# Norm factors folded into small per-token scalars, and another order of loads, splits and modulation matmuls at six seams of a two-layer backbone

## The chip, the cores and the metric

One core of a Trainium2 chip runs the whole program. The metric is the device time in microseconds (us), the median of the timed executions shown below. TensorE is named PE in the profile, VectorE DVE, ScalarE ACT, GpSimd POOL; SP is the engine whose queue issues most loads and stores.

## The reference, cut to what matters

512 tokens (256 context, 256 latent) of width 1024 pass through two layers. What the change touches of each layer:

```python
ml = adaln(c, w_ada[l], b_ada[l])                # six modulation rows: shift, scale, gate, twice
hl = modulate(rmsnorm(xl, norm1_g[l]), ml[0], ml[1])
# token mixing: three branches of one input projection, merged by sigmoid gates
q = rmsnorm(q, qn_g); k = rmsnorm(k, kn_g)       # (A) attention, per head half of 64
s = q @ k.T * 64 ** -0.5;  p = softmax(s)
q = l2norm(q) * 128 ** -0.5;  k = l2norm(k)      # (B) gated DeltaNet, per head of 128
kb = k * beta;  l_mat = strict(kb @ k.T * decay) # then a chunked scan with q, k, v, beta, g
y = rmsnorm(o, norm_g) * silu(z)
y = gates[0] * (ys[0] @ w_branch[0]) + gates[1] * (ys[1] @ w_branch[1]) + gates[2] * (ys[2] @ w_branch[2])
xl = xl + ml[2] * (y @ w_out)
hl = modulate(rmsnorm(xl, norm2_g[l]), ml[3], ml[4])
xl = xl + ml[5] * peer_ffn(hl, ...)              # product-key experts
```

Layer 1 needs the latent tokens alone behind its keys and values, so most of its blocks are 256 columns wide where layer 0 has 512.

## The kernel before, in words

Activations lie transposed, features on partitions and tokens along the free dimension. Each matrix product is three fp32r matmuls (`mm3`, L101 to L103): the operand is split into a high part (an ACT cast, L94) and a rest (a DVE subtraction, L97). `wblock` (L119) loads one weight block of 512 KB and splits it; `tblock` (L133) multiplies it with the hidden state `hh`, `hl`.

`run` (L1289) goes through a layer in this order. **Start**: `norm_sums` (squares and column sums of x), the modulation blocks (`ada`, L175: four loads of 512 KB, 8 matmuls on the two condition vectors, a copy on ACT, a fold of four small matmuls), the small parameters (`mix_params`), then `hmod` (L203), which takes the reciprocal root of the sums, spreads it over the partitions by two matmuls (`rowb`, L499 and L500) and makes `hh` and `hl`. **Mixer** (L226): `gdn_gates`, then `weave` mixes three streams of work: the DeltaNet groups (two heads each, `gdn_group`), the recurrent and attention heads with `merge_early` behind them, and a list of fillers, merge gates and `ada` blocks. How many units of the others follow each DeltaNet unit is a table (`RATE`, L267), which the change leaves alone. **Merge** (L930): the DeltaNet branch output, which lies in memory as `ysd[1]`, is loaded (`yraw`), split and projected, summed with the other two (`y`, `ya`) under the gate `mth`, and projected with `w_out` onto x. **Second norm**: `hmod` again with `ada` blocks 10 and 11. Then queries, routing and experts.

Norm factors in the mixer are per token, and a token is a column there. `cols_rsqrt` leaves them as one column of scalars per 128 tokens; `rowsb` (L461) spreads such columns to a full tile by one 128x128 fp32 matmul per 128 tokens (L470), and DVE multiplies. `sq_cols` (L448) forms the sums of squares by an ACT square and one matmul with one column out per 128 tokens (L454).

The engines work their rows in order; the recording layer places the rows of each engine. The DMA queue of SP takes loads in the order of its rows. Weight loads share three buffers (`wraw`).

## Time and profile before

| what | value |
|---|---|
| time, median of 3 runs | 4547.12 us (4546.77 to 4556.1) |
| time of the profiled execution | 4536.66 us |
| its span | 4535.0 us |
| mean granted TensorE clock | 0.969 of 2.4 GHz |
| busy: PE, DVE, ACT, POOL | 4283.0 (94%), 3214.4 (71%), 2348.0 (52%), 457.7 (10%) us |

The profiled execution is 10.5 us shorter than the median, so sums are made against 4536.66 and carried over to 4547.12. The stretches of its span, in us: start 0 to 65, mixer of layer 0 to 1177, merge to 1294, second norm to 1322, queries, routing and experts to 2606; start of layer 1 to 2648, mixer to 3550, merge to 3622, second norm to 3641, the rest to 4535. Busy shares are averages over these; at the borders PE stands still. Those borders are called seams here.

### The profile page before, as it was taken

The page shows a single profiled execution, that of the slowest core. Times are in us where ns is not written, and L with a number is a line of the kernel's source. Part 1 is how long each engine was busy: PE and PEld are TensorE (multiplying, and loading weights), DVE is VectorE, ACT ScalarE, POOL GpSimd, SP SyncE. Part 2 cuts the span into 40 slices and gives each one's busy share as a digit, 9 for nine tenths or more (in the row PEclk, how much of TensorE's full clock was granted, in tenths as well). Part 3 has the DMA queues.
Part 4 walks back from the last instruction along what each step waited for, and adds up shares of the span by engine and source line. Part 5 has one row for each costly group of instructions (what it writes and reads, how often), then busy time and mean ns, then how long its engine had stood idle before and what let it go on. Part 6 is the DMA issues. An engine that isn't in the chain of part 4 may idle for free.

```text
span 4535.0 us, 67054 instructions
## 1 busy us (share of the span) xinstructions
PE 4283.0 (94%) x24379; PEld 3612.7 (80%) x24379; DVE 3214.4 (71%) x7412; ACT 2348.0 (52%) x4145; POOL 457.7 (10%) x444
## 2 busy tenths in 40 slices
PE   7999999999889999999999989989998899999999
PEld 4686877777668999988888856878776789988888
DVE  4767576764459998677888766777775588656665
ACT  4555555553244688433333354656554357854444
POOL 0000000000000222333444200000000001100000
PEclk8999999999989999999999989999998999999999
DMA  4313222225632688899999734223221746677775
GB/s 152 121 59 109 70 96 86 96 73 175 205 107 91 235 275 294 320 333 336 338 340 333 251 121 140 84 84 98 66 89 57 236 149 208 228 266 243 242 248 182
DMA packets 364604, 820.69 MB, mean 181 GB/s; under 512 B 67184, under 2 KB 187504, under 8 KB 360944
## 3 DMA queue, kind: packets, MB, share of 16 engines
q1 hardware_dynamic: 315568, 614.00, 41.4%
q0 software_dynamic: 45824, 160.46, 9.7%
q10 hardware_dynamic: 2880, 41.94, 2.4%
q8 instruction: 191, 3.13, 0.3%
q14 instruction: 141, 1.16, 0.1%
HBM read 715.62 MB, written 100.66 MB: 180 GB/s over the span
## 4 chain that ended last, share of the span: by engine, by line
PE 81%; DVE 10%; ACT 4%; DMA 4%; issue 1%; SPq 0%; ACTq 0%; DVEq 0%
PE mm L103 11%; PE mm L101 11%; PE mm L102 11%; PE acx L101 4%; PE acx L102 4%; PE acx L103 4%; PE px L101 3%; PE px L102 3%; PE px L103 3%; DVE wl L97 2%; PE acg L103 1%; PE acg L101 1%; PE px L872 1%; PE acg L102 1%; PE pg L102 1%; PE pg L101 1%
## 5 line engine op out<-in xcount | busy, mean ns | idle before, releaser
L101 PE MATMUL mm<-hh,wh 128*128 128x256 f32 (+2 forms) x2784 | 916.2, 329 | 38.9 <-ACT wh L94 26.7
L103 PE MATMUL mm<-hh,wl 128*128 128x256 f32 (+2 forms) x2784 | 908.9, 327 | 18.6 <-DVE wl L97 18.3
L102 PE MATMUL mm<-hl,wh 128*128 128x256 f32 (+2 forms) x2784 | 903.5, 325 | 0.0
L94 ACT CAST wh<-wraw 128x1024 fp32r<-128x1024 f32 (+2 forms) x473 | 487.6, 1033 | 660.6 <-PE mm L102 525.2
L97 DVE TENSOR_TENSOR wl<-wraw,wh 128x1024 fp32r<-128x1024 f32 (+2 forms) x473 | 566.8, 1199 | 231.9 <-ACT wh L94 229.8
L101 PEld LDWEIGHTS mm<-hh,wh 128*128 128x128 f32 x2784 | 533.2, 192 | 68.9 <-ACT wh L94 28.5
L103 PEld LDWEIGHTS mm<-hh,wl 128*128 128x128 f32 x2784 | 531.9, 191 | 49.3 <-DVE wl L97 29.9
L102 PEld LDWEIGHTS mm<-hl,wh 128*128 128x128 f32 x2784 | 533.2, 192 | 22.9 <-issue 2.5
L97 DVE TENSOR_TENSOR vl<-vraw,vh 128x1024 fp32r<-128x1024 f32 x256 | 313.0, 1223 | 142.3 <-ACT vh L94 139.6
L94 ACT CAST vh<-vraw 128x1024 fp32r<-128x1024 f32 x256 | 269.0, 1051 | 274.4 <-PE pg L103 164.7
L94 ACT CAST pah<-ge 128x384 fp32r<-128x384 f32 (+1 forms) x256 | 114.7, 459 | 225.3 <-DVE ge L1196 172.0
L1160 DVE TENSOR_SCALAR ob<-cst,iT 128x128 f32<-128x128 f32 x640 | 183.3, 347 | 66.1 <-PE pg L1161 22.1
L1013 POOL DMA_DIRECT2D early<-ge x160 | 89.3, 558 | 1355.5 <-ACT ge L1006 952.3
L1218 POOL DMA_INDIRECT grow<-in_v,gix x128 | 179.5, 1403 | 259.4 <-DVE gacc L1233 229.6
L101 PE MATMUL mm<-hh,whx 128*128 128x512 f32 (+1 forms) x544 | 202.9, 373 | 2.9 <-ACT tx L800 1.8
L103 PE MATMUL mm<-hh,wlx 128*128 128x512 f32 (+1 forms) x544 | 200.9, 369 | 2.1 <-DVE wlx L97 2.1
L102 PE MATMUL mm<-hl,whx 128*128 128x512 f32 (+1 forms) x544 | 201.3, 370 | 0.0
L101 PE MATMUL px<-vh,pah 128*128 128x512 f32 x512 | 199.5, 390 | 0.0
L102 PE MATMUL px<-vl,pah 128*128 128x512 f32 x512 | 199.5, 390 | 0.0
L103 PE MATMUL px<-vh,pal 128*128 128x512 f32 x512 | 199.2, 389 | 0.0
L1218 POOL DMA_INDIRECT grow<-in_ur,gix x128 | 161.4, 1261 | 269.8 <-DVE gdot L1224 163.0
L1233 DVE SCALAR_TENSOR_TENSOR gacc<-grow,gdot,gacc 128x1024 f32<-128x1024 f32 x127 | 163.3, 1286 | 1.5
(518 smaller groups left out, 10030.3 us busy)
## 6 DMA issues: line engine op xcount, KB each, us to landing
wraw<-in_u SPq DMA_DIRECT2D x256, 512.0 KB
vraw<-in_v SPq DMA_DIRECT2D x256, 512.0 KB
wraw<-in_win SPq DMA_DIRECT2D x192, 512.0 KB
wraw<-in_wada SPq DMA_DIRECT2D x96, 512.0 KB
gate<-st ACTq DMA_DIRECT2D x20, 2048.0 KB
wraw<-in_wbr SPq DMA_DIRECT2D x48, 512.0 KB
pgt<-gate SPq DMA_DIRECT2D x32, 768.0 KB
wraw<-in_wq SPq DMA_DIRECT2D x32, 512.0 KB
```

The source lines that it names most:

```text
L94: self.S.copy(h, src)
L97: return self.V.tensor_tensor(l, src, h.bitcast(F32), ALU.subtract)
L101: mm(out, lh, rh, start=first, stop=False)
L102: mm(out, lh, rl, start=False, stop=False)
L103: mm(out, ll, rh, start=False, stop=last)
L872: T.matmul(sc, a[s, q0:q0 + P], b[s, :nk], start=t == 0, stop=t == 2)
L1013: self.nc.gpsimd.dma_start(hd[j], self.expert_h(gl, l, j, T0, N))
L1160: ob = V.tensor_scalar(b, iota, iT[:, 1, n + k:n + k + 1], iT[:, 2, n + k:n + k + 1], ALU.is_equal, ALU.mult)
L1218: nc.gpsimd.indirect_dma_start(r, None, table, bass.IndirectOffsetOnAxis(ap=ix[:, k:k + 1], axis=0))
L1233: V.scalar_tensor_tensor(acc, r, dot[:, k:k + 1], acc, ALU.mult, ALU.add)
```

## The change

**DeltaNet.** The keys stay raw: their squared norm factor goes into beta (`bt`, `nbt`, `nb0`, 8 or 16 columns wide), its root into the value tile (`dv`, by a DVE multiply in place of an ACT copy). The query factor goes into the epsilon of the output norm (`qe`), since that norm divides it out again. The output `o` is formed with tokens on partitions (`qg` and `QK` become the weights of its matmuls), so the output norm's factor is a scalar per partition: ACT squares 128 columns at a time with a running sum, ACT scales 128 columns at a time, PE transposes back, and one DVE operation in place of two applies gain and gate. The blocks of a group come as k0, k1, q0, v0, q1, v1.

**Attention.** The query gain is applied by the ACT copy out of PSUM, and the query factor times 0.125 is the softmax scale, so that queries need no `rowsb`.

**Seams.** The first load of x is in 8 parts; the modulation blocks at the start have 8 buffers of their own. The gate weights and the first weight block behind each `hmod` are loaded and split ahead of it. Blocks 4, 5 and 10, 11 (of both layers) come as a `fill` behind the second `rowb` matmul; blocks 4 and 5 of layer 0 leave the mixer's filler list for that. In `merge` the loads of `yraw` come first, then `ya`, then x; `yraw` has 4 buffers in layer 0 and 8 in layer 1.

```diff
+    def preload(self, dram):
+
+        self.pre = self.wblock(dram)
...
+        if self.pre:
+            w, self.pre = self.pre, None
+            return w
...
-            w = self.t(self.wp, [P, 2, 512], F32, "wraw", 3)
+            w = self.t(pool, [P, 2, 512], F32, "adaw", 8) if pool else self.t(self.wp, [P, 2, 512], F32, "wraw", 3)
...
+        fp = self.tc.tile_pool(name=self.nm("fill"), bufs=1, reuse_waits="tile")
+        with fp as p, self.tc.issue_after(self.lastrow.ins):
+            for b in fill:
+                self.ada(l, b, p)
...
-            ad = [lambda a=a: self.ada(*a) for a in ([(0, b) for b in range(4, 10)] + [(1, b) for b in range(4)] if l == 0 else [(1, b) for b in range(6, 10)])]
+            ad = [lambda a=a: self.ada(*a) for a in ([(0, b) for b in range(6, 10)] + [(1, b) for b in range(4)] if l == 0 else [(1, b) for b in range(6, 10)])]
...
+            if w < 2:
+                self.sq_cols(dst, ss[:, sc[w][hh]:], self.ones[:, :1])
+            if w:
+                pt = self.px()
+                for c in range(4):
+                    T.transpose(pt[:, c * P:(c + 1) * P], dst[:, c * P:(c + 1) * P], idt)
+                if w == 1:
+                    S.copy(kN[:, hh].rearrange("p a b -> p (a b)"), pt)
                 else:
-                    dst = (kT if w else qT)[:, hh]
-                    V.scalar_tensor_tensor(dst, th, 1.0, cv, ALU.add, ALU.mult)
-                    self.sq_cols(dst, ss[:, sc[w][hh]:], self.ones[:, :1])
+                    V.tensor_tensor(vN[:, hh], v4(pt), dv[:, 4 * hh:4 * hh + 4].unsqueeze(2).to_broadcast([P, 4, P]), ALU.mult)
+            if (hh, w) == (1, 1):
+                k2, dv = c1("k2"), c1("dv")
+                V.tensor_scalar(k2, ss[:, :8], 1.0, 4 * EPS, ALU.mult, ALU.add)
+                rk = self.rsqrt(self.sp, k2, "rq")
+                V.scalar_tensor_tensor(dv, k2, 0.5, rk, ALU.mult, ALU.mult)
+                V.tensor_tensor(k2, rk, rk, ALU.mult)
+                bt, nbt, nb0 = mk([P, 2, 4, 2], "bt", F32, 2), mk([P, 2, 4, 2], "nbt", F32, 2), mk([P, 2, 4], "nb0", F32, 2)
+                two = lambda ap: ap.rearrange("p c (d h) -> p h c d", h=8)[:, 2 * g:2 * g + 2]
+                V.tensor_tensor(bt, two(self.bN), k2.rearrange("p (h c) -> p h c", c=4).unsqueeze(3).to_broadcast([P, 2, 4, 2]), ALU.mult)
+                V.tensor_scalar(nbt, bt, -1.0, None, ALU.mult)
+                V.tensor_tensor(nb0, two(self.neg)[:, :, :, 0], bt[:, :, :, 0], ALU.mult)
+            yield "in"
+            if w == 2:
                 yield "in"
-        rs = self.cols_rsqrt(ss[:, :8 + 2 * nq], 1.0, 4 * EPS)
-        V.tensor_scalar(rs[:, 8:], rs[:, 8:], 128 ** -0.5, None, ALU.mult)
-        for hh in range(2):
-            for w in range(2):
-                t0 = T0 if w == 0 else 0
-                dst = (qT, kT)[w][:, hh]
-                o = sc[w][hh]
-                V.tensor_tensor(dst, dst, self.rowsb(rs[:, o:o + (4 if w else nq)], 1), ALU.mult)
-            pt = self.px()
-            for c in range(4):
-                T.transpose(pt[:, c * P:(c + 1) * P], kT[:, hh, c * P:(c + 1) * P], idt)
-            S.copy(kN[:, hh].rearrange("p a b -> p (a b)"), pt)
-            yield "in"
+        qe = c1("qe", 2 * nq)
+        V.tensor_scalar(qe, ss[:, 8:8 + 2 * nq], P * EPS, 4 * P * EPS * EPS, ALU.mult, ALU.add)
...
+                    V.scalar_tensor_tensor(W[:, hd * 4 + c], pkk[:, c], nbt[:, hh, c, d:d + 1], Ws[d][:, c], ALU.mult, ALU.mult)
                 V.tensor_tensor(QK[:, hd], QK[:, hd], pkq[:, c0:], ALU.mult)
...
                 if si:
-                    T.matmul(po, s0, qg[:, hd, c - c0], start=True, stop=False)
-                T.matmul(po, vn, QK[:, hd, c - c0], start=si == 0, stop=True)
+                    T.matmul(po, qg[:, hd, c - c0], s0, start=True, stop=False)
+                T.matmul(po, QK[:, hd, c - c0], vn, start=si == 0, stop=True)
...
         yield "fin"
-        so = self.acc()
+        so = c1("so", 2 * nq)
         for hh in range(2):
-            self.sq_cols(qT[:, hh], so[:, nq * hh:], self.ones[:, :1])
-        rs = self.cols_rsqrt(so[:, :2 * nq], 1.0 / P, EPS)
+            sq = self.r([P, N])
+            for c in range(nq):
+                cs = slice(c * P, (c + 1) * P)
+                S.activation(sq[:, cs], qT[:, hh, cs], AF.Square, accum_out=so[:, nq * hh + c:nq * hh + c + 1])
+        V.scalar_tensor_tensor(so, so, 1.0 / P, qe, ALU.mult, ALU.add)
+        rs = self.rsqrt(self.sp, so, "rq")
         yield "fin"
...
-            V.scalar_tensor_tensor(y, qT[:, hh], self.gng, self.rowsb(rs[:, nq * hh:nq * (hh + 1)], 1), ALU.mult, ALU.mult)
-            V.tensor_tensor(y, y, th, ALU.mult)
-            nc.sync.dma_start(self.ysd[1][:, h, T0:], y)
+            pt = self.px()
+            for c in range(nq):
+                cs = slice(c * P, (c + 1) * P)
+                S.activation(y[:, cs], qT[:, hh, cs], AF.Copy, scale=rs[:, nq * hh + c:nq * hh + c + 1])
+                T.transpose(pt[:, cs], y[:, cs], idt)
+            V.scalar_tensor_tensor(th, pt[:, :N], self.gng, th, ALU.mult, ALU.mult)
+            nc.sync.dma_start(self.ysd[1][:, h, T0:], th)
...
-            S.copy(raw[:, w, t0:], ps[:, :NTOK - t0])
-            self.sq_cols(raw[:, w, t0:], ss[:, 8 - 8 * w:], self.C["selh"][:, 6:8])
+            if w:
+                S.copy(raw[:, w], ps)
+            else:
+                S.activation(raw[:, w, t0:], ps[:, :N], AF.Copy, scale=self.qkg[:, 0:1])
+            self.sq_cols(raw[:, w] if w else ps[:, :N], ss[:, 8 - 8 * w:], self.C["selh"][:, 6:8])
...
+        rq = mk([P, 2 * nq], "rq8", F32, 2)
+        V.tensor_scalar(rq, rs[:, 8:], 0.125, None, ALU.mult)
...
-            pb = self.rowsb(rs[:, :8] if w else rs[:, 8:], 2)
...
-            V.scalar_tensor_tensor(x[:, t0:], x[:, t0:], self.qkg[:, w:w + 1], pb, ALU.mult, ALU.mult)
+            if w:
+                V.scalar_tensor_tensor(x, x, self.qkg[:, w:w + 1], self.rowsb(rs[:, :8], 2), ALU.mult, ALU.mult)
...
-                    V.tensor_scalar(sm[:, 2 + c:3 + c], sm[:, c:c + 1], -0.125, None, ALU.mult)
+                    r8 = rq[:, 2 * (q0 - T0) // P + c:2 * (q0 - T0) // P + c + 1]
+                    V.tensor_scalar(sm[:, 2 + c:3 + c], sm[:, c:c + 1], r8, -1.0, ALU.mult, ALU.mult)
...
-                    S.activation(e, sc, AF.Exp, scale=0.125, bias=sm[:, 2 + c:3 + c], accum_out=sm[:, 4 + c:5 + c])
+                    S.activation(e, sc, AF.Exp, scale=r8, bias=sm[:, 2 + c:3 + c], accum_out=sm[:, 4 + c:5 + c])
...
+            yh, yl = pair()
+            for c in range(8):
+                raw = mk([P, N], "yraw", F32, 8 * NC // N)
+                nc.sync.dma_start(raw, self.ysd[1][:, c, T0:])
+                self.split(yh[:, c], yl[:, c], raw)
             for d in range(8):
                 nc.sync.dma_start(ya[:, d], self.yad[2][:, d])
-            yh, yl = pair()
-            for c in range(8):
-                raw = mk([P, N], "yraw", F32, 3)
-                nc.sync.dma_start(raw, self.ysd[1][:, c, T0:])
-                self.split(yh[:, c], yl[:, c], raw)
+            nc.sync.dma_start(x, xd)
...
-        nc.sync.dma_start(x, self.I["xT"])
+        for k in range(8):
+            nc.sync.dma_start(x[:, k], self.I["xT"][:, k])
...
-                        self.ada(l, b)
+                        self.ada(l, b, p)
...
-                    self.ada(l, 4)
-                    self.ada(l, 5)
-                self.hmod(p, x, "n1g", l, 0, 1, 0)
+                self.gate_weights(l)
+                self.preload(self.I["win"][l, B_BK])
+                self.hmod(p, x, "n1g", l, 0, 1, 0, (4, 5))
...
-            nc.sync.dma_start(x, self.I["xT"] if l == 0 else xd)
-            if need:
-                self.mix_params(self.par, l + 1)
...
-                self.ada(l, 10)
-                self.ada(l, 11)
-                self.hmod(p, x, "n2g", l, 3, 4, T0)
+                if need:
+                    self.mix_params(self.par, l + 1)
+                self.preload(self.I["wq"][l, 0])
+                self.hmod(p, x, "n2g", l, 3, 4, T0, (10, 11))
```

The places in the order at which this shows best are three. First SP's queue where the merge of layer 0 begins; `yraw` is the DeltaNet output, `ya` and `y` the other two branches, `mth` the gate, `wraw` weights. Before:

```order
L121 DMA wraw_10051<-in_wbr 128x1024
L1320 DMA x_9822<-in_xT 128x4096
L939 DMA ya_9888<-yad_9185 128x512 x8
L943 DMA yraw_9899<-ys_98_422 128x512
L943 DMA yraw_9903<-ys_98_422 128x512
L943 DMA yraw_9907<-ys_98_422 128x512
L948 DMA y_1887_9932<-yad_9500 128x512
L951 DMA mth_9935<-mg_420 128x512
L943 DMA yraw_9911<-ys_98_422 128x512
```

After the change:

```order
L972 DMA yraw_9747<-ys_119_495 128x512
L972 DMA yraw_9751<-ys_119_495 128x512
L972 DMA yraw_9755<-ys_119_495 128x512
L972 DMA yraw_9759<-ys_119_495 128x512
L975 DMA ya_9744<-yad_9100 128x512
L972 DMA yraw_9763<-ys_119_495 128x512
L972 DMA yraw_9767<-ys_119_495 128x512
L972 DMA yraw_9771<-ys_119_495 128x512
L972 DMA yraw_9775<-ys_119_495 128x512
L975 DMA ya_9744<-yad_9100 128x512 x7
L976 DMA x_9737<-in_xT 128x4096
L980 DMA y_1860_9789<-yad_9415 128x512
```

The eight loads of `yraw` stand ahead of seven of the eight `ya`, and x stands behind all of them; `y` and `mth` are behind x in both.

Second PE's rows at the start of layer 0, from the last modulation block to the first gate matmul (L101). Before:

```order
L185 MATMUL mm_247<-wraw_248,csil 32x512 x2
L185 MATMUL mm_247<-wraw_252,csil 32x512 x2
L185 MATMUL mm_247<-wraw_256,csil 32x512 x2
L185 MATMUL mm_247<-wraw_260,csil 32x512 x2
L190 MATMUL mm_266<-fold,wl_264 128x2 x4
L101 MATMUL acx_436<-hh_368,wh_432 32x512
L102 MATMUL acx_436<-hl_369,wh_432 32x512
L103 MATMUL acx_436<-hh_368,wl_433 32x512
```

After:

```order
L199 MATMUL mm_273<-fold,arow_271 128x2 x4
L194 MATMUL mm_390<-adaw_391,csil 32x512 x2
L194 MATMUL mm_390<-adaw_395,csil 32x512 x2
L194 MATMUL mm_390<-adaw_399,csil 32x512 x2
L194 MATMUL mm_390<-adaw_403,csil 32x512 x2
L199 MATMUL mm_409<-fold,arow_407 128x2 x4
L194 MATMUL mm_415<-adaw_416,csil 32x512 x2
L194 MATMUL mm_415<-adaw_420,csil 32x512 x2
L194 MATMUL mm_415<-adaw_424,csil 32x512 x2
L194 MATMUL mm_415<-adaw_428,csil 32x512 x2
L199 MATMUL mm_434<-fold,arow_432 128x2 x4
L101 MATMUL mm_503<-hh_441,wh_339 32x512
```

Two more modulation blocks (`mm_390`, `mm_415`, the fill) stand between the last block of before and the gate matmuls.

Third PE's rows in the first DeltaNet group, where the last block of a group ends and the decay rows (L499, after: L509) begin; `pg` are the group's PSUM tiles. Before:

```order
L551 MATMUL pg_893<-cst,kT_527 128x128 x4
L470 MATMUL pg_899<-cst,rqy_867 128x128 x4
L470 MATMUL pg_905<-cst,rqy_867 128x128 x4
L454 MATMUL px_1174<-cst,tx_1207 128x2 x4
L101 MATMUL mm_1213<-hh_368,whx_1216 128x512
L102 MATMUL mm_1213<-hl_369,whx_1216 128x512
L103 MATMUL mm_1213<-hh_368,wlx_1217 128x512
L101 MATMUL mm_1213<-hh_368,whx_1216 128x512
L551 MATMUL pg_911<-cst,kT_527 128x128 x4
L499 MATMUL pg_954<-Gh_511,identR 128x512
```

After:

```order
L101 MATMUL mm_1172<-hh_441,wh_1175 128x512
L102 MATMUL mm_1172<-hl_442,wh_1175 128x512
L103 MATMUL mm_1172<-hh_441,wl_1176 128x512
L551 MATMUL pg_952<-cst,tg_950 128x128 x4
L509 MATMUL pg_997<-Gh_576,identR 128x512
L510 MATMUL pg_997<-Gl_577,identR 128x512
L101 MATMUL mm_1172<-hh_441,wh_1175 128x512
L102 MATMUL mm_1172<-hl_442,wh_1175 128x512
L509 MATMUL pg_1017<-Gh_576,identR 128x512
L510 MATMUL pg_1017<-Gl_577,identR 128x512
```

The `rowsb` matmuls (L470) and the second pass of transposes (L551 of before) are gone from there; the transposes of v (L551 of after) are the last rows of the group's blocks.

## Rows read from the trace of the kernel before

**Rows 1.** Profile page, part 4: chain of work that ended last, by engine.

```profile
PE 81%; DVE 10%; ACT 4%; DMA 4%; issue 1%; SPq 0%; ACTq 0%; DVEq 0%
```

**Rows 2.** Windows: span; busy PE, PEld, DVE, ACT, POOL; PEclk, DMA share, GB/s.

```profile
65.00:1177.00 1112.00, 1082.95 (x5797) 841.60 (x5796) 732.56 (x1727) 568.50 (x1085) 11.75 (x11) 0.98 0.31 101
1177.00:1212.00 35.00, 14.73 (x49) 9.97 (x49) 14.35 (x32) 7.43 (x11) 0.00 (x0) 0.71 0.83 285
...
2648.00:3550.00 902.00, 831.24 (x5094) 689.95 (x5092) 635.19 (x1548) 498.25 (x957) 11.89 (x11) 0.94 0.31 97
```

**Rows 3.** Timeline of PE at the start of layer 0.

```profile
49.91 1.87 PE L190 MATMUL mm<-fold,wl 128*128 128x2 f32 x8 [0.74 <-ACT wl L187]
64.67 0.64 PE L101 MATMUL acx<-hh,wh 128*32 128x512 f32 x1 [12.89 <-ACT wh L94]
```

**Rows 4.** Timeline of PE at the second norm of layer 0.

```profile
1307.25 0.39 PE L500 MATMUL px<-hr,identR 8*128 8x512 f32 x1
...
1321.47 0.79 PE L101 MATMUL mm<-hh,wh 128*128 128x512 f32 x1 [9.12 <-ACT wh L94]
```

**Rows 5.** Timeline of PE at the start of layer 1.

```profile
2632.57 0.79 PE L500 MATMUL px<-hr,identR 8*128 8x512 f32 x1
...
2647.62 0.63 PE L101 MATMUL mm<-hh,wh 128*32 128x512 f32 x1 [10.74 <-ACT wh L94]
```

**Rows 6.** Timeline at the merge of layer 0: SP's queue, then PE.

```profile
1181.08 0.42 SPq L1320 DMA_DIRECT2D x<-in_xT  x1
1181.61 8.15 SPq L939 DMA_DIRECT2D ya<-yad  x8
1190.83 1.64 SPq L943 DMA_DIRECT2D yraw<-ys  x3
...
1196.89 0.80 PE L101 MATMUL mm<-yh,wh 128*128 128x512 f32 x1 [19.43 <-ACT yh L94]
```

**Rows 7.** Timeline at the merge of layer 1: PE, then SP's queue.

```profile
3564.24 0.58 PE L101 MATMUL mm<-yh,wh 128*128 128x256 f32 x1 [16.32 <-ACT yh L94]
...
3551.07 9.56 SPq L939 DMA_DIRECT2D ya<-yad  x8
```

**Rows 8.** Groups by form, 70 to 1130 us: busy us, mean ns, idle before.

```profile
L185 PE MATMUL mm<-wraw,csil 128*32 128x512 f32 x112 | 29.2, 677 | 8.3 <-DMA wraw<-in_wada 8.3
...
L470 PE MATMUL px<-cst,tx 128*128 128x128 f32 x128 | 19.5, 285 | 0.0
...
L185 PE MATMUL acx<-wraw,csil 128*32 128x512 f32 x48 | 12.2, 604 | 3.5 <-DMA wraw<-in_wada 3.5
...
L190 PE MATMUL mm<-fold,wl 128*128 128x2 f32 x72 | 10.2, 262 | 3.6 <-ACT wl L187 3.6
L451 ACT ACTIVATE tg<-qT 128x512 f32<-128x512 f32 x16 | 10.0, 627 | 7.6 <-DVE qT L538 3.9 <-DVE qT L646 3.7
L573 ACT ACTIVATE rg<-pg,nGn 128x128 f32<-128x128 f32 x32 | 9.1, 366 | 12.8 <-DVE rqy L111 7.0 <-DVE rg L568 5.9
```

**Rows 9.** Chain in order of time, 130 to 150 us: start, us, what.

```profile
140.82 0.44 PE pg L551 x4
141.25 1.83 PE pg L470 x16
```

**Rows 10.** Timeline of PE near 91 us.

```profile
90.95 1.05 PE L454 MATMUL acg<-ones,tg 128*128 128x1 f32 x8
```

**Rows 11.** Group by form in the mixer of layer 0: ACT reading a running sum.

```profile
L877 ACT ACTIVATION_READ_ACCUMULATOR tx<-px,asm 128x1 f32 x64 | 12.5, 195 | 0.0
```

**Rows 12.** Timeline of PE at the second norm of layer 1.

```profile
3637.34 1.05 PE L185 MATMUL mm<-wraw,csil 128*32 128x512 f32 x4 [1.88 <-DMA wraw<-in_wada]
```

**Rows 13.** Timeline of DVE at the start: first and last of a root's operations.

```profile
25.99 0.19 DVE L484 TENSOR_SCALAR rqx<-px 128x32 f32<-128x32 f32 x1 [1.41 <-PE px L482]
...
28.46 0.19 DVE L116 SCALAR_TENSOR_TENSOR rqy<-rqs,rqy 128x32 f32<-128x32 f32 x1
```

**Rows 14.** What PE waited for before L470 in the mixer of layer 1: us, times.

```profile
  DVE rqy L116: 38.0, 11
```

More of the change, by code (lines that the diff above doesn't have):

```diff
@@ L185, in ada @@
                 T.matmul(ps[q:q + 32], self.cs[:, j], w[:, i], start=j < 4, stop=j >= 4)
-        row = self.t(self.wp, [P, 512], F32, "wl", 2)
+        row = self.t(pool or self.wp, [P, 512], F32, "arow" if pool else "wl", 2)
         self.S.copy(row, ps)
@@ L201, in norm_sums, with hmod @@
             self.ssq(x[:, k, t0:], self.nss[:8, :NTOK - t0], self.selR[:, 7:15], k == 0, k == 7)
-    def hmod(self, pool, x, gname, l, mshift, mscale, t0):
+    def hmod(self, pool, x, gname, l, mshift, mscale, t0, fill):
         V, S = self.V, self.S
@@ L375, in softplus, with gate_weights @@
         V.scalar_tensor_tensor(p, p, 2.0, e, ALU.mult, ALU.add)
+    def gate_weights(self, l):
+        raw = self.t(self.wp, [P, 8, 32], F32, "wraw", 3)
+        self.nc.sync.dma_start(raw, self.I["wba"][l])
+        self.wba = self.t(self.wp, [P, 8, 32], F32R, "wh", 2), self.t(self.wp, [P, 8, 32], F32R, "wl", 2)
+        self.split(*self.wba, raw)
     def gdn_gates(self, mp, l):
@@ L382, in gdn_gates @@
         idt = self.C["ident"]
[L383 to L386 removed]
+        wh, wl = self.wba
         ps = self.mm()
@@ L415, in gdn_gates @@
         self.split(self.Gh, self.Gl, pb[:16])
-        V.tensor_scalar(self.nbN, self.bN, -1.0, None, ALU.mult)
         V.tensor_scalar(self.nGn, self.Gn, -1.0, None, ALU.mult)
         S.activation(self.edl, self.edl, AF.Exp)
-        S.activation(eg, self.Gn, AF.Exp)
-        for d in range(2):
-            ed = eg[:, :, 8 * d:8 * d + 8]
-            if d == 0:
-                V.scalar_tensor_tensor(self.nbe[:, :, 0:8], ed, -1.0, self.bN[:, :, 0:8], ALU.mult, ALU.mult)
-            else:
-                V.tensor_scalar(self.nbe[:, :, 8:16], ed, -1.0, None, ALU.mult)
+        S.activation(self.neg, self.Gn, AF.Exp)
+        V.tensor_scalar(self.neg, self.neg, -1.0, None, ALU.mult)
     def conv(self, ps, w, n, seg0, out, bias=None):
@@ L541, in gdn_group @@
[L541 to L553 removed]
+            t0 = T0 if w == 0 else 0
@@ new lines, in gdn_group @@
+            n = NTOK - t0
+            if hh == 0 and w == 0:
+                qT = mk([P, 2, N], "qT")
+            ps = self.mm()
+            self.tblock(ps[:, :n], I["win"][l, (B_BQ, B_BK, B_BV)[w] + h], t0)
+            cv, th = self.r([P, n]), self.r([P, n])
+            self.conv(ps, self.gcw[:, 8 * w + h], n, t0 // NC, cv)
+            S.activation(th, cv, AF.Tanh, scale=0.5)
+            dst = self.r() if w == 2 else (kT if w else qT)[:, hh]
+            V.scalar_tensor_tensor(dst, th, 1.0, cv, ALU.add, ALU.mult)
@@ L621, in gdn_group @@
                 R2 = sl("R")
-                V.scalar_tensor_tensor(R2, b[:, 0:P], self.nbe[:, c, hc], R, ALU.mult, ALU.add)
+                V.scalar_tensor_tensor(R2, b[:, 0:P], self.neg[:, c, hc] if d else nb0[:, hh, c:c + 1], R, ALU.mult, ALU.add)
                 R = R2
@@ L928, in merge_early, with merge @@
                 yield
-    def merge(self, l, x, npool):
+    def merge(self, l, x, xd, npool):
         nc, V, S, I = self.nc, self.V, self.S, self.I
```

41 lines of the change are left out of this document (10 added, 31 removed).

## The prediction

> **What bounds the kernel now.** I read the chain of the page first. PE holds 81% of it, DVE 10%, ACT and DMA 4% each [rows 1], so the time falls where PE has less to do or stands still for less. The windows by stage then say where which of the two holds [rows 2]. In the mixer of layer 0 PE is busy 1082.95 of 1112 us, DVE 732.56, ACT 568.50: work taken from PE there counts in full. In the mixer of layer 1 PE is busy 831.24 of 902 us: most of it counts. At the seams PE stands still. In the 35 us at the merge of layer 0 it is busy 14.73 us while the DMA engines are 83% busy, and the granted clock falls to 0.71, so the matmuls behind a gap run partly at 1.2 GHz too. The timelines give what ends each gap: the weight cast on ACT, queued behind `hmod`'s work, at the starts and at the second norm of layer 0 (12.89, 10.74 and 9.12 us) [rows 3, 4, 5], the split of `yraw` at the merges (19.43 and 16.32 us) [rows 6, 7].
>
> **Folded norms in the mixer of layer 0.** An fp32 matmul has two records (8 heads x 8 matmuls show as 128 [rows 8]). The chain passes 16 records of L470 in 1.83 us, so one `rowsb` matmul of 128 columns costs 0.229 us, and four transposes take 0.44 us, 0.11 each [rows 9]. Eight records of L454, four matmuls with one column out, take 1.05 us, 0.26 each [rows 10]. What goes:
> - 64 `rowsb` matmuls for DeltaNet q and k: 64 x 0.229 = 14.7 us
> - 32 for attention q: 7.3 us
> - 32 one-column matmuls of the output norm: 32 x 0.26 = 8.4 us
> - 32 `rowsb` matmuls of the output norm become 32 transposes: 32 x 0.12 = 3.8 us
>
> That is 34 us. Two modulation blocks leave the fillers too. Ten blocks have 29.2 + 12.2 us of matmuls there and nine folds 10.2 us [rows 8], so 4.1 + 1.1 us a block, and 11.8 us of waiting for weights [rows 8] with 3.6 us for the copy add 1.6: 6.9 us at most, 4.1 at least. I take 6, 12 us for the two (bounds 8 and 14). Layer 0's mixer: -46.
>
> DVE loses the multiplies by spread factors and gains the value multiply and some small operations, about even. ACT gains most. A square of 512 columns takes 0.627 us, and an operation on 128 columns 0.366 [rows 8] with 0.195 for reading its running sum [rows 11]: four squares take 2.24 us, and the four scalings of 128 columns another 1.46. That is 3.1 us more per head, 25 us over eight heads, less the value copies. ACT would then be busy about 590 of 1112 us [rows 2], so I cost it at nothing; what hides it is PE's work on the other streams. If PE stood waiting for it, the cost would be that of the third rival.
>
> The Trainium skill's page "ScalarE: Activation LUTs" (What ACT_TABLE_LOAD costs) speaks against cutting an operation into four: each activation with a pointer operand has a fixed part of about 0.28 us beside 0.83 ns an element. By it a piece of 128 takes 0.39 us, which the row (0.366) bears out; the sum would be the same by either, and what the rule threatens is the third rival.
>
> **The same in layer 1.** Queries are 256 columns there: 48 matmuls for q and k (11.0 us), 16 for attention q (3.7), 16 one-column matmuls (4.2), 16 changed to transposes (1.9), 20.8 us in all. With PE busy 92% of the stage I take 17 (bounds 8, if the waits of that stage fill in, and 21).
>
> **The seams.**
> - Start of layer 0: the last fold starts at 49.91 and the first gate matmul at 64.67, behind its weight cast, which on ACT stands behind seven of `hmod`'s eight rounds [rows 3]. With eight buffers the 16 weight blocks stream. As rate I take 4.2 MB (x and `ya`) from 1181.08 to about 1196 [rows 6], 0.28 MB/us: 8.4 + 2.1 MB take 37 us, so the last fold ends near 43 and `hmod`'s ACT work some 8 us sooner. The fill, two blocks of 4.2 MB, takes 15 us more to land, to about 53, and is ahead of the gates on PE. Gates near 58: -7 (bounds -2, -10).
> - Merge of layer 0: SP issues x at 1181.08, `ya` until 1189.8, `yraw` from 1190.83, and PE starts at 1196.89 [rows 6]. With `yraw` first in the queue, the load and the split take what they take now, some 6 us less the transfers still ahead of them. I put the first matmul at 1184: -13 (bounds -6, -16).
> - Second norm of layer 0: the second spread matmul is at 1307.25, the first query matmul at 1321.47, after 9.12 us of waiting for its weight cast [rows 4]. The cast is to be done ahead, and without modulation blocks in between the spread comes near 1304. The fill then takes two times 6 us on PE: 1316, -6 (bounds 0, -10).
> - Start of layer 1: spread at 2632.57, gates at 2647.62 [rows 5]. Likewise 2630 + 12 = 2642, and the clock is less fallen: -7 (bounds -2, -12).
> - Merge of layer 1: `ya` is issued from 3551.07 on for 9.56 us ahead of `yraw`, PE starts at 3564.24 [rows 7]. `yraw` first saves those 9.56: -10 (bounds -5, -13).
> - Second norm of layer 1: the blocks stand behind the spread already; eight buffers save the wait of 1.88 [rows 12] and its like: -3 (bounds 0, -6).
>
> Sum of the seams: -46 (bounds -15 and -67). All at one end is not likely; I use -25 and -62.
>
> **The sum.** -46 - 17 - 46 = -109 on 4536.66 makes 4428 for an execution like the profiled one. The median of the runs shown stands 10.5 us higher, and carried over to it the sum makes 4547 - 109 = 4438. With the bounds (-38 to -48 and -8 to -21 in the mixers, seams as said) it goes from -71 to -131: 4416 to 4476.
>
> **The rivals.**
> 1. *The gaps only move.* In the merge `y` and `mth` now stand behind x. 6.3 MB from 1181 on at 0.28 MB/us land near 1203, and DVE frees no PSUM tile before. PE has four tiles of 24 matmuls to fill, about 6 us each, so it lasts until about 1207; if the loads are later, PE stops there instead. The fill may also hold up the first block, since PE takes its rows in order. For it speaks the 83% DMA share [rows 2], against it that x was wanted late. Seams at half: 4461. The Trainium skill's "DMA: Bandwidth & Descriptors" (Queues, rings and completion order) says that each DMA engine takes the descriptors of one ring in order. The trace agrees: `yraw`, issued 10 us behind x, was first used at 1196.89. By it `y` and `mth` cannot pass x either.
> 2. *Layer 1's mixer gives nothing* for the fold, since PE's 71 us of idle there hang on ACT and DVE. Against it: the chain is PE's. 4455.
> 3. *Slower.* The output norm becomes a longer chain ahead of PE rows: squares on ACT, the root on DVE, a scaling on ACT, then the transposes, which PE takes in order. Alone, eight squares with sums (4.5 us), the root (2.7 [rows 13]) and a first scaling with its neighbours (1.5) are 8.7 us. There are 16 heads. If PE waited the whole chain at each, 16 x 8.7 = 139 us come back, 4577 in the end; it decides from 6.8 us a head. For it speaks that L470 already waited 38.0 us in 11 places for such a root [rows 14]; against it that many rows of the other streams lie between the stages of this chain. At those rows' 3.5 us a head, 56 us come back: 4494.
> 4. *The fill does not fill.* Its weights come only after the seam's other loads, and PE waits in front of the first block: the four norm seams give nothing, 4461 again.
>
> **How the numbers follow.** Forecast, 4438: 0.55. Seams at half, by the first or the fourth: 0.2. Layer 1 nothing: 0.1. Waits for the output norm at 3.5 us: 0.1. The full third rival: 0.05. The range 4400 to 4495 holds all but the last and little at its ends: at the low end 16 us beyond the bounds, for gaps whose end also spares matmuls at 1.2 GHz. About 0.2% is what a measurement of this kernel can tell from no change. Faster by that: 0.93; the same 0.02, slower 0.05, both out of the third rival.
>
> **What would show it.** Right: no L470 from DeltaNet q and k; PE busy in the first mixer down by 40 to 50 us with the span of that stage; the first `yraw` matmul within 8 us of the last matmul of the mixer; the first block behind each norm starting as soon as the second fold is done, and no weight cast ahead of it. Wrong: PE waiting for ACT before the transposes of the output norm for more than 3 us each, DVE waiting for `mth` with PE idle some 20 us into the merge, a fill block waiting for its weights, or a mixer whose span does not shrink with PE's work.

## The result, and the profile after

The change makes the kernel faster: 4484.67 us (median of 4, 4476.8 to 4491.95) against 4547.71 us (4 runs, 4546.77 to 4556.1), ratio 0.986 [0.984, 0.988], -63 us. Forecast were 4438 us, -109, with a range of 4400 to 4495. The sign and the range held; the size is little over half.

The profiled execution took 4490.03 us. Part 4 of its page, the chain by engine, against [rows 1]:

```profile
PE 77%; DVE 12%; ACT 5%; DMA 4%; issue 2%; SPq 0%; ACTq 0%; DVEq 0%
```

Windows of the two mixers and of the 35 us at the merge, with the columns of [rows 2]:

```profile
58.00:1154.00 1096.00, 1064.46 (x5462) 818.25 (x5460) 714.46 (x1716) 579.63 (x1152) 11.17 (x11) 0.97 0.30 98
1154.00:1189.00 35.00, 27.08 (x102) 20.46 (x103) 16.16 (x23) 10.21 (x15) 0.00 (x0) 0.85 0.83 282
2607.00:3506.00 899.00, 816.43 (x4926) 673.46 (x4926) 622.16 (x1549) 508.05 (x995) 12.88 (x12) 0.93 0.30 94
```

The merge is what it was to be: PE works 27.08 of 35 us instead of 14.73. The mixers are not. The first lost 335 of 5797 matmul records and 16 us of length, the second 168 of 5094 and only 3, and PE stands still there for 82.57 us where it stood for 70.76. In all the span went from 4535.0 to 4488.3 us, -47 where -109 was forecast: -16 of -46 in layer 0's mixer, -3 of -17 in layer 1's, -28 of -46 at the seams. The median gained more, since the execution of before that was profiled had a high clock (0.969). Timeline of PE at the seams, against [rows 3 to 7]:

```profile
50.29 1.05 PE L199 MATMUL mm<-fold,arow 128*128 128x2 f32 x8 [2.14 <-ACT arow L196]
...
56.44 1.54 PE L199 MATMUL mm<-fold,arow 128*128 128x2 f32 x8 [2.99 <-ACT arow L196]
57.84 0.61 PE L101 MATMUL mm<-hh,wh 128*32 128x512 f32 x1
...
1161.34 0.80 PE L101 MATMUL mm<-yh,wh 128*128 128x512 f32 x1 [7.69 <-ACT yh L94]
...
1272.87 0.79 PE L510 MATMUL px<-hr,identR 8*128 8x512 f32 x1
1273.59 3.64 PE L194 MATMUL mm<-adaw,csil 128*32 128x512 f32 x16
1277.93 1.87 PE L199 MATMUL mm<-fold,arow 128*128 128x2 f32 x8 [0.70 <-ACT arow L196]
1279.73 3.64 PE L194 MATMUL mm<-adaw,csil 128*32 128x512 f32 x16
...
1285.83 0.78 PE L101 MATMUL mm<-hh,wh 128*128 128x512 f32 x1
...
2606.84 0.50 PE L101 MATMUL acx<-hh,wh 128*128 128x512 f32 x1
...
3513.85 0.58 PE L101 MATMUL mm<-yh,wh 128*128 128x256 f32 x1 [7.75 <-ACT yh L94]
```

No weight cast ends a gap any more: behind each norm the first block follows the fill at once, and the merges wait 7.7 us instead of 19.43 and 16.32. But behind the second norm of layer 0 the fill's 12.2 us run at 1.2 GHz: the granted clock is 0.50 from 1273.6 to 1285.8, and 16 of its records take 3.64 us, where those of an earlier block take 1.92 at a clock of 0.99 (at 34.94 us in this trace).

**A measure for the clock.** Each run lists its span and the mean granted TensorE clock. Span x clock is called net time here, span x (1 - clock) the clock deficit; the two add up to the span. The clock has three digits, so one execution's net is known to some 2 us. Net time is not work alone, since idle time is in it at its own clock. So for a stage the deficit is counted on busy time: PE's busy time x (1 - clock), summed over windows of 10 us; busy time less this is called the stage's work. One kernel's executions scatter in the deficit: over the eight of the changed kernel (e12 among them) the standard deviation is 11 us, and differences of less than 10 to 14 us between two kernels are not clear of that. All runs, the time as median, net and deficit as means over executions (the edits are in the next section):

| kernel | time, us | ratio to before | net | deficit |
|---|---|---|---|---|
| before | 4542 to 4548 | | 4386 to 4388 | 153 to 160 |
| changed | 4484.67 | 0.9859 [0.9843, 0.9875] | 4319 | 164 |
| e12, changed, again | 4484.69 | 0.9873 [0.9853, 0.9894] | 4321 | 163 |
| e1, folds alone | 4514.83 | 0.9934 [0.9913, 0.9955] | 4346 | 167 |
| e2, seams alone | 4496.15 | 0.9902 [0.988, 0.9924] | 4360 | 136 |
| e9, seams + DeltaNet fold | 4477.0 | 0.9856 [0.9839, 0.9872] | 4327 | 148 |
| e10, seams + attention fold | 4497.3 | 0.9896 [0.9879, 0.9912] | 4358 | 137 |
| e3, matmuls put back | 4491.05 | 0.9885 [0.9864, 0.9906] | 4342 | 147 |
| e4, output norm of before | 4487.29 | 0.9874 [0.985, 0.9899] | 4334 | 151 |
| e5, merge of before | 4500.91 | 0.9892 [0.9874, 0.991] | 4326 | 173 |
| e6, x late | 4492.98 | 0.9872 [0.9853, 0.9892] | 4323 | 166 |
| e7, no fill at norm 2 | 4487.68 | 0.9871 [0.9851, 0.9891] | 4324 | 162 |
| e8, gaps filled | 4474.22 | 0.9847 [0.9824, 0.9869] | 4329 | 146 |
| e11, e8 + e9 | 4472.58 | 0.9843 [0.9819, 0.9866] | 4327 | 145 |

### The profile page after: what moved, and what is told of

Its sections match the earlier page's. It is cut to its first block, busy times and chain, and to the rows that moved or that the text cites. A ratio compares the mean times of both kernels' runs of the same rounds, so it can differ in the third digit from the quotient of the medians.

```text
span 4488.3 us, 66242 instructions
## 1 busy us (share of the span) xinstructions
PE 4254.6 (95%) x23915; PEld 3579.6 (80%) x23915; DVE 3186.7 (71%) x7416; ACT 2369.0 (53%) x4246; POOL 463.1 (10%) x444
## 4 chain that ended last, share of the span: by engine, by line
PE 77%; DVE 12%; ACT 5%; DMA 4%; issue 2%; SPq 0%; ACTq 0%; DVEq 0%
PE mm L103 11%; PE mm L102 11%; PE mm L101 11%; PE acx L103 4%; PE acx L102 4%; PE acx L101 4%; PE px L102 3%; PE px L101 3%; PE px L103 3%; DVE wl L97 2%; PE px L902 1%; PE acg L101 1%; PE acg L103 1%; PE acg L102 1%; PE mm L194 1%
## 5 line engine op out<-in xcount | busy, mean ns | idle before, releaser
L101 PE MATMUL mm<-hh,wh 128*128 128x256 f32 (+3 forms) x2912 | 972.7, 334 | 15.3 <-ACT wh L94 7.9
L103 PE MATMUL mm<-hh,wl 128*128 128x256 f32 (+3 forms) x2912 | 966.2, 332 | 19.9 <-DVE wl L97 19.8
L102 PE MATMUL mm<-hl,wh 128*128 128x256 f32 (+3 forms) x2912 | 961.6, 330 | 0.0
L103 PEld LDWEIGHTS mm<-hh,wl 128*128 128x128 f32 (+1 forms) x2912 | 557.7, 192 | 57.6 <-DVE wl L97 29.3
L101 PEld LDWEIGHTS mm<-hh,wh 128*128 128x128 f32 (+1 forms) x2912 | 558.6, 192 | 50.1 <-ACT wh L94 9.6
L102 PEld LDWEIGHTS mm<-hl,wh 128*128 128x128 f32 (+1 forms) x2912 | 559.1, 192 | 27.2 <-issue 1.4
L101 PE MATMUL px<-vh,pah 128*128 128x512 f32 x512 | 199.6, 390 | 0.0
L101 PE MATMUL mm<-hh,whx 128*128 128x512 f32 (+1 forms) x448 | 161.7, 361 | 11.3 <-ACT tx L825 10.7
L103 PE MATMUL mm<-hh,wlx 128*128 128x512 f32 (+1 forms) x448 | 160.7, 359 | 1.9 <-DVE wlx L97 1.9
L102 PE MATMUL mm<-hl,whx 128*128 128x512 f32 (+1 forms) x448 | 159.7, 356 | 0.0
```

The costliest lines, as they stand in the source:

```text
L101: mm(out, lh, rh, start=first, stop=False)
L102: mm(out, lh, rl, start=False, stop=False)
L103: mm(out, ll, rh, start=False, stop=last)
```

## The experiments

The theories after the result, with the letters of the expectations: PE's work went, but the granted clock fell with it and took part of the gain back (A). PE is bound and removed work counts in full, as predicted (B). PE meets new waits, behind the cut pieces of the output norm on ACT, or in layer 1's mixer behind ACT and DVE (C).

**e1 and e2: each half alone.** e1 is the kernel before with `gdn_group`, `att_head` and the factors of `gdn_gates` as changed; e2 is the changed kernel with these three as before. Against the changed kernel, the core of e1, then of e2:

```diff
-                self.gate_weights(l)
-                self.preload(self.I["win"][l, B_BK])
-                self.hmod(p, x, "n1g", l, 0, 1, 0, (4, 5))
+                self.hmod(p, x, "n1g", l, 0, 1, 0)
```

```diff
-                V.tensor_tensor(nb0, two(self.neg)[:, :, :, 0], bt[:, :, :, 0], ALU.mult)
...
+        rs = self.cols_rsqrt(ss[:, :8 + 2 * nq], 1.0, 4 * EPS)
+        V.tensor_scalar(rs[:, 8:], rs[:, 8:], 128 ** -0.5, None, ALU.mult)
```

> The kernel before with the folded norms of DeltaNet and attention alone; seams and fillers as before. Theory A (the clock takes it back): the matmuls dropped in the mixers leave less for PE to do between its waits, the granted clock falls there, and most of the work saved is lost again: 10 to 30 us less than before, the loss by the clock in the mixer of layer 0 above 30 us of full-speed time where before has 17. Theory B (PE bound, as predicted): 34 + 17 = 51 us less, ratio near 0.989, clock as before. Theory C (new waits behind ACT's cut pieces): 10 to 30 us less as in A, but with PE idle time in the mixers up by 20 us or more and the clock about as before.

> The changed kernel with the norms of DeltaNet and attention queries as before; seams, fill and fillers as changed. If the parts add up, this and the fold alone make the 63 us together. Theory A: 35 to 50 us less than before, 12 of them from the two modulation blocks that leave the mixer, the rest from the start, the two merges and the start of layer 1; the second norms give nothing. The prediction's own terms ask for 46 + 12 = 58 us less, ratio 0.987.

The seams with the two blocks bring 49 us where 58 were forecast, the folds 30 alone and on top of the seams 12 by the medians, 20 by the ratios, where 51 were. So B falls. By net time the folds are worth 40 both times (4386 to 4346, 4360 to 4320). What differs is the deficit: the seams lower it from 156 to 136, and the folds raise it again to 163. In e1's profile A and C are both there: in layer 0's mixer the deficit on busy time is 25 us where before has 15, and idle time 36 where it has 29; in layer 1's idle time is 81 where it has 69, and the deficit no higher (37, before 44).

**e3: the dropped matmuls put back, for nothing.** 112 matmuls whose result nobody reads, one for each `rowsb` matmul dropped from DeltaNet q and k.

```diff
                 pt = self.px()
+                for c in range(4 if w == 1 else nq):
+                    T.matmul(pt[:, c * P:(c + 1) * P], self.C["ident"], self.C["ident"], start=True, stop=True)
                 for c in range(4):
```

> The changed kernel with 112 matmuls put back that nobody needs (identity by identity, 128 columns in fp32, in PSUM that the next transposes write over), in the blocks of k and v where the spreading matmuls were dropped. They wait for nothing new. At 0.229 us each they are 25.6 us of PE work. Theory B: 20 to 26 us more than the changed kernel, ratio to before near 0.991. Theory A: 0 to 10 us more, since the clock rises with them; loss by the clock in the two mixers down by 10 us or more from 37 and 66. Theory C: somewhere between 0 and 26, clock unchanged, idle time down.

Their price is 112 x 0.229 = 25.6 us, the net time rises by 23, the time by 6 (by the scatter of the executions between nothing and 14). That is less than B asks for. It is A's sign: 25 us of matmuls, with no dependence but their place in PE's row, cost about a quarter of their length, and the deficit is 16 us lower (2 to 30 by the scatter). Where it falls is not shown. In e3's profile layer 0's mixer, with 64 of the 112, is 1115.9 us long (1095.8 and 1095.3 in the two profiles of the changed kernel), layer 1's 887.9 (899.3 and 888.0), and the deficit on busy time in both together is 69 (80 and 69).

**e4: the output norm of before in the changed kernel**, squares and sums on PE again, `rowsb`, two multiplies on DVE.

```diff
-                S.activation(sq[:, cs], qT[:, hh, cs], AF.Square, accum_out=so[:, nq * hh + c:nq * hh + c + 1])
+            self.sq_cols(qT[:, hh], so[:, nq * hh:], self.ones[:, :1])
...
-                T.transpose(pt[:, cs], y[:, cs], idt)
+            V.scalar_tensor_tensor(y, qT[:, hh], self.gng, self.rowsb(rs[:, nq * hh:nq * (hh + 1)], 1), ALU.mult, ALU.mult)
```

> The changed kernel with the output norm of DeltaNet as before (squares over full rows, one-column matmuls, spread factors); keys, queries and seams stay changed. It puts back 48 one-column matmuls and 48 spreading ones for 48 transposes, 12.5 + 5.8 = 18 us of PE work, and takes 96 short operations from ACT. Theory B: 18 us more than the changed kernel. Theory A: 8 us more to 8 less. Theory C: 10 us or more less, with the wait of the attention transposes for DVE in the mixer of layer 1 (10.8 us, before 0.8) down again.

The new chain costs nothing: without it the kernel is no faster, and in layer 1's mixer PE's idle time stays (79.8 us), as does the wait of the attention transposes (11.2 us). C falls as far as this chain goes, and so does B, which asked for 18 us more.

**e5: the merge order of before.**

```diff
+            for d in range(8):
+                nc.sync.dma_start(ya[:, d], self.yad[2][:, d])
...
-            for d in range(8):
-                nc.sync.dma_start(ya[:, d], self.yad[2][:, d])
-            nc.sync.dma_start(x, xd)
```

> The changed kernel with the order of loads in both merges as before: x first, then the other branches, then the DeltaNet output with three buffers. By the prediction's terms the two gaps of 7.7 us grow back to 19.4 and 16.3 us and the merges behind them gain nothing: 20 us more than the changed kernel (ratio to before near 0.990). If what the gaps gained came back inside the merges, as the first rival had it, 0 to 8 us more: the traces show 134.8 us from the first merge matmul to the queries before and 135.2 after in layer 0, 83.6 and 87.8 in layer 1.

16 us are given back by the medians (7 to 25 by the scatter); the first wait of layer 0's merge is 18.27 us again. **e6: x behind the gates.**

```diff
-            nc.sync.dma_start(x, xd)
             for d in range(8):
...
+            nc.sync.dma_start(x, xd)
             yh, yl = pair()
```

> The changed kernel with the load of x behind the last gate load of the merge, ahead of the splits for the output projection. If gates and branch loads queued behind x hold the merges up (PE waited 2.0 us for a gate's tile in layer 1, and the merges there took 4 us longer than before), 3 to 8 us less than the changed kernel. If the merges are slower for another reason, 0, and if x now comes too late for the output projection, more.

No gain. In the merge of layer 1 PE waits 2.0 us for `mth` in the changed kernel; in e6 that wait is gone, but PE's waits for split weights grow from 3.3 to 8.8 us. **e7: blocks 10 and 11 ahead of the second norm again.**

```diff
+                self.ada(l, 10)
+                self.ada(l, 11)
...
-                self.hmod(p, x, "n2g", l, 3, 4, T0, (10, 11))
+                self.hmod(p, x, "n2g", l, 3, 4, T0, ())
```

> The changed kernel with modulation blocks 10 and 11 of both layers ahead of the second norm as before, no fill there; the first weight block is still split ahead. By the prediction's term the fill is worth 9 us in the two second norms. By the traces it was worth nothing (the fill ran at 1.2 GHz for 13 us, because PE had been waiting ahead of it): within 4 us of the changed kernel, or a little less time.

The same time within the intervals: the fill at the second norm is worth nothing that can be measured. In e7's profile it is even dearer in layer 0: with the blocks ahead of the norm, in the waits of its sums and its root, and the weights still split ahead, the first query matmul starts 116.3 us behind the first merge matmul (at 1162.85), with the fill 124.5. In layer 1 both are 80.

```profile
1279.19 0.77 PE L101 MATMUL mm<-hh,wh 128*128 128x512 f32 x1
```

**e8: PE's gaps filled with matmuls that nobody needs**, while a root is formed and while the merge waits.

```diff
+        pw = self.px()
+        for k in range(20):
+            T.matmul(pw[:, :P], self.identR, self.identR, start=True, stop=True)
         y = self.rsqrt(self.sp, x, "rq")
...
+            pw = self.px()
+            for k in range(48):
+                self.T.matmul(pw[:, :P], self.identR, self.identR, start=True, stop=True)
             yh, yl = pair()
```

> The changed kernel with matmuls that nobody needs in gaps in which PE waits: 20 of 128 columns while each norm's root is formed on DVE (4 places), 48 at the start of each merge. They lie in waits and delay nothing by the trace. If what PE does ahead of a piece of work sets the clock of that piece, the fills, which took 2 x 6.2 us at 1.2 GHz, and the first matmuls of the merges run at 2.4 GHz: 8 to 20 us less than the changed kernel, and the granted clock of the stages around the seams (0.86, 0.76 and 0.84 in the windows that hold them) up. If the clock goes by something else: 0, or a few us more.

More work, not more time: net +9, deficit -17, 10 us less by the medians. The interval overlaps that of the changed kernel, so a gain is not shown; that the added work, which lies in PE's waits, costs nothing is. Of the clock the expectation was half met: in the fill behind the second norm of layer 0 the second block takes 1.92 us instead of 3.64, the first still 3.64.

**e9 and e10: one fold undone.** The changed kernel with `att_head` as before (e9), or with `gdn_group` and the factors of `gdn_gates` as before (e10, the second diff of e2). The core of e9:

```diff
-        V.tensor_scalar(rq, rs[:, 8:], 0.125, None, ALU.mult)
...
+            pb = self.rowsb(rs[:, :8] if w else rs[:, 8:], 2)
...
-                    S.activation(e, sc, AF.Exp, scale=r8, bias=sm[:, 2 + c:3 + c], accum_out=sm[:, 4 + c:5 + c])
+                    S.activation(e, sc, AF.Exp, scale=0.125, bias=sm[:, 2 + c:3 + c], accum_out=sm[:, 4 + c:5 + c])
```

> The changed kernel with the attention queries spread and scaled as before (DeltaNet and seams as changed). Asked: which of the two folds adds the 12 us of PE's idle time in the mixer of layer 1 (68.7 us before, 82.5 after). If the attention's (its softmax chain then hangs on DVE behind the exponentials, which PE waits for: 10.8 us before the probabilities' transposes, 10.7 us for the scaled query): idle in that mixer 68 to 72, and the time equal to the changed kernel's or below, 4470 to 4486, though 11 us of matmuls are back. If DeltaNet's: idle stays near 80 and the time is 4486 to 4496.

> The changed kernel with DeltaNet as before, the attention fold and the seams kept. The counterpart: 37.6 us of matmuls by the prediction's prices are back. If the attention's fold makes the idle time of layer 1's mixer: idle near 80 there, and a time at or above that of the kernel with both folds undone (4496): 4494 to 4506. If DeltaNet's: idle 68 to 72 and 4488 to 4496. If the granted clock gives most of any matmul work back, net time (span times clock) up by about 25 us but the time by 15 at most.

Each run came out as if its own fold made the idle time: it is 68 to 70 us in both, though the two expectations were to exclude each other. The windows of layer 1's mixer, first e9, then e10, then the changed kernel once more (e12):

```profile
2609.00:3497.00 888.00, 819.96 (x4958) 674.75 (x4958) 626.56 (x1553) 508.00 (x1003) 13.14 (x12) 0.93 0.31 95
```

```profile
2632.00:3518.00 886.00, 815.88 (x5074) 675.02 (x5070) 626.12 (x1548) 505.35 (x963) 12.87 (x12) 0.95 0.31 95
```

```profile
2604.00:3492.00 888.00, 804.76 (x4929) 665.17 (x4926) 622.94 (x1552) 508.06 (x995) 13.00 (x12) 0.94 0.30 95
```

Idle are 68.0, 70.1 and 83.2 us: either fold alone leaves it near the 68.7 of before, and both together raise it (80.5 in e1, which has both too). What PE waits for there, in the changed kernel (us in total, times, longest):

```profile
PE px L480 <- DVE rqy L116: 17.1, 4, 4.9
PE px L916 <- DVE tx L913: 10.8, 4, 3.4
PE mm L101 <- ACT tx L825: 10.7, 1, 10.7
```

and in e9:

```profile
PE px L480 <- DVE rqy L116: 15.4, 4, 5.1
PE mm L101 <- ACT tx L825: 8.9, 2, 6.5
PE px L910 <- DVE tx L907: 6.9, 4, 3.5
```

L916 (e9: L910) transposes the softmax's difference, L101 behind `tx` is the recurrent head's product. The reading, not tried by an edit, is that PE comes to the same waits sooner with less to do between them; these three make up 7 of the 15 us. In time the attention fold is worth nothing that shows (e2 to e10: 4496 to 4497; e9 to the changed kernel: 4477 to 4485, intervals overlapping), and the DeltaNet fold all of it (e2 to e9: 0.9902 to 0.9856, 21 us; e10 to the changed kernel 13). e10 also bears A out: 37.6 us of matmuls are back, net time is 38 us up, and the time 13 (4 to 19 by the scatter). The DeltaNet fold holds the new order of a group's blocks too; no run has one without the other.

**e11 and e12: both edits of e8 and e9, and the changed kernel beside them on the same chip.**

```diff
+            pb = self.rowsb(rs[:, :8] if w else rs[:, 8:], 2)
...
+        for k in range(20):
+            T.matmul(pw[:, :P], self.identR, self.identR, start=True, stop=True)
```

> The changed kernel with the attention queries as before and with matmuls that nobody needs in PE's gaps (20 of 128x128 while a group's or head's root is formed, 48 while the merge waits for its first split). If the two gains add, the attention fold undone (8 us, 4477 against 4485) and the filled gaps (8 to 10 us): 4466 to 4472, ratio to the kernel before 0.982 to 0.984, faster than the changed kernel by an interval that leaves zero out. If both only give back the same clock deficit (163 us in the changed kernel, 148 and 146 in the two): 4473 to 4480, no better than either alone.

> The changed kernel unaltered, on the same chip as the one with both edits, for a direct comparison: 4480 to 4490, net time (span times clock) 4319, clock 0.962 to 0.966. Both theories say the same of it.

4472.58 against 4484.69 us: 12 less, with 18 us less deficit. The gains don't add: the deficit is 145 us where e8 and e9 each have 146 and 148. The intervals of e11 and e12 overlap. It is the lowest time found, but that it beats the changed kernel is not shown.

## Why the prediction was right in sign and too large

**The step that failed** is the first: "PE is busy 1082.95 of 1112 us [...]: work taken from PE there counts in full." Most of the priced work went. From e2 to the changed kernel the folds take layer 0's mixer from 1060.5 to 1032.6 us of work, -28, forecast -34, and layer 1's from 786.6 to 769.1 (770.5 in e12), -17, priced at -21. But layer 0's stage gets only 11.5 us shorter (1107.3 to 1095.8), and layer 1's 8 us longer or 3 shorter (891.1 to 899.3, in e12 888.0). The windows of the two mixers in e2:

```profile
58.00:1165.00 1107.00, 1080.23 (x5750) 843.42 (x5748) 729.77 (x1713) 567.66 (x1079) 11.05 (x11) 0.98 0.30 97
2618.00:3509.00 891.00, 823.25 (x5104) 686.43 (x5101) 631.18 (x1548) 502.35 (x968) 12.98 (x12) 0.95 0.30 95
```

In layer 0 it is mostly the clock: the deficit on busy time rises from 20.0 to 32.0 us (e12: 34.6), idle time from 26.8 to 31.2. In layer 1 it is the waits first: idle time rises from 67.7 to 82.5 us (e12: 83.2), while the deficit rises from 36.8 to 47.6 in the first profile but not in e12 (34.3). That is C. The forecast did allow for it, "bounds 8, if the waits of that stage fill in", and the bound was still too high. Rival 2 (layer 1 gives nothing) had the place right, and the sign named for being wrong, "a mixer whose span does not shrink with PE's work", came true there.

Two more terms were too large. The two blocks that left layer 0's mixer were to save 12 us; from before to e2 that stage is 5.5 shorter (1112.8 to 1107.3). The seams are told below. No term had the clock of the mixers in it. That the range held is in part luck: the highest sum by the bounds was 4476, and 4484.67 lies above it, in the room left for the third rival, whose wait did not come.

That the clock is what differs shows best where nothing else does. Two profiles of the changed kernel, the first and e12, have the same sequence of 4926 records in layer 1's mixer (the windows count 4926 and 4929) and the same idle time, but busy times of 816.43 and 804.76 us. Windows near one place, of the first:

```profile
2780.00:2800.00 20.00, 20.00 (x95) 16.61 (x96) 6.03 (x22) 4.95 (x11) 0.00 (x0) 0.56 0.11 40
```

and of e12:

```profile
2780.00:2800.00 20.00, 20.00 (x146) 16.43 (x144) 10.01 (x32) 12.46 (x40) 0.00 (x0) 1.00 0.00 1
```

Both say PE was busy all the time, and the granted clock says that the first was mostly at 1.2 GHz. They hold not quite the same rows, since e12 is already ahead; but the 94 matmuls that start in the first's window took it 20.1 us, and the same 94 took 12.3 in e12 (2773.84 to 2786.12). These 8 us are most of the 11 by which the two mixers differ. A full busy row is thus no sign that PE works at full speed. In the first profile PE was busy 18.16 of the 20 us before that window, in e12 18.98.

**ACT at no cost** was right: 579.63 us busy, forecast 590, and hardly a wait of PE before the transposes of the output norm (0.7 us in 3 places over both layers). Groups by form in layer 0's mixer, ACT's square and scaling, then PE's transposes:

```profile
L689 ACT ACTIVATE tg<-qT,rqy 128x128 f32<-128x128 f32 x32 | 10.5, 398 | 0.0
...
L675 ACT ACTIVATE tg<-qT 128x128 f32<-128x128 f32 x32 | 9.7, 305 | 4.0 <-DVE qT L663 4.0
```

```profile
L690 PE MATMUL pg<-cst,tg 128*128 128x128 f32 x32 | 7.6, 295 | 0.0
```

The Trainium skill's "ScalarE: Activation LUTs" (What ACT_TABLE_LOAD costs) tells an activation with a pointer operand (0.28 us fixed) from one with immediates (0.19). The trace agrees: 398 ns for the scaling by a pointer, 305 for the square. The forecast priced both at 0.366. The third rival needed 3.5 us a head; it fell. The 38.0 us it was argued from [rows 14] count PE and its weight loads together; the waits of PE alone there were 18.6 us in 5 places.

**The merges.** The gaps were sized right: 19.43 to 7.69 and 16.32 to 7.75, -20 for -23. The order of SP's queue in the changed kernel, against [rows 6]:

```profile
1156.21 1.80 SPq L972 DMA_DIRECT2D yraw<-ys  x4
1158.05 0.43 SPq L975 DMA_DIRECT2D ya<-yad  x1
1162.04 2.33 SPq L972 DMA_DIRECT2D yraw<-ys  x4
1164.42 3.86 SPq L975 DMA_DIRECT2D ya<-yad  x7
1169.15 0.33 SPq L976 DMA_DIRECT2D x<-in_xT  x1
```

x goes 13 us behind the first `yraw`, `y` and `mth` behind x. In layer 0 this costs little. In layer 1 the first rival came true in part: the spread of the second norm (second matmul of `rowb`) starts 63.4 us behind the first merge matmul in the kernel before and 63.9 in e5, but 67.2 in the changed kernel (69.6 in e12), so 4 to 6 of the 8.6 us come back. The spread in layer 1, of before, of the changed kernel and of e5 (first merge matmul at 3564.24, 3513.85 and 3541.07):

```profile
3627.64 0.38 PE L500 MATMUL px<-hr,identR 8*128 8x256 f32 x1
```

```profile
3581.05 0.58 PE L510 MATMUL px<-hr,identR 8*128 8x256 f32 x1
```

```profile
3605.02 0.58 PE L510 MATMUL px<-hr,identR 8*128 8x256 f32 x1
```

That leaves 15 us for the two merges, as e5's 16 say. PE waits for `mth` and for split weights there, and e6 shows that moving x alone does not cure it; what would stays open.

**The second norms** gave nothing, forecast -6 and -3. From the first merge matmul to the first query matmul are 124.5 us in layer 0 (1161.34 to 1285.83) and were 124.6 [rows 4, 6]; in layer 1 they are 79.9 and were 76.6, which is the merge's loss. In layer 0 the spread did not come earlier (111.5 us behind that matmul, 110.4 before), so the fill's 12.2 us only took the place of the wait for the cast; by e7's profile the cast ahead would have saved 8 us without it. Its weights were there in time, so rival 4's wait is not what happened; "two times 6 us" was right, "near 1304" for the spread was not.

**The starts**: -4 in layer 1 for -7 (-7 in e12, where the second block of the fill took 1.92 us), and in layer 0 -7 as forecast in this profile, though a block of the fill waited 4.66 us for its weights there. It is not so in each profile. Of the twelve profiles of kernels with the new start, nine have the first gate matmul at 57 to 61 us and three (e5, e6, e9) at 67 to 68, no earlier than before. PE's timeline in e6:

```profile
59.88 1.86 PE L199 MATMUL mm<-fold,arow 128*128 128x2 f32 x8 [7.68 <-ACT arow L196]
61.68 3.55 PE L194 MATMUL mm<-adaw,csil 128*32 128x512 f32 x16
66.03 1.05 PE L199 MATMUL mm<-fold,arow 128*128 128x2 f32 x8 [0.80 <-ACT arow L196]
```

and its windows:

```profile
20.00:30.00 10.00, 7.77 (x33) 2.46 (x35) 3.03 (x14) 1.73 (x3) 0.00 (x0) 0.70 0.88 340
30.00:40.00 10.00, 9.19 (x33) 2.84 (x29) 4.94 (x9) 0.59 (x1) 0.00 (x0) 0.50 0.44 129
```

The granted clock fell at 20 to 30 us there (in the changed kernel's own profile it is 1.00 in that window), the blocks ran late, and the fold of the fill waited 7.68 us for its copy on ACT, which was busy 8.34 of the 10 us from 50 on.

**The carry-over to the median** was a matter of the clock too: the profiled execution of before had 0.969 where the mean of its runs is 0.965.

What stays open: why both folds together, and neither alone, bring the 13 to 15 us of idle time in layer 1 was read from the waits and not tried by an edit of its own, such as another table of the mix. Nor is it shown what in the folds makes the clock fall in layer 0, the missing matmuls or the new order of the blocks; e3, which puts matmuls back, lowers the deficit of the whole but not of that stage.
